# A hybrid encoder layer on one core: rows of a block's inverse dealt out in turn, two more merge columns computed in pairs, two output half columns begun early

## The chip, the core and the metric

The kernel runs on one core of a Trainium2 chip as one program. The metric is device time of one launch in microseconds (us). The core's engines are TensorE (PE, with its weight loads as PEld), VectorE (DVE), ScalarE (ACT) and GpSimd (POOL); SyncE (SP) issues most of the transfers between the chip's memory and the core, POOL a few of them. Each engine works through its own list of instructions in order and waits for the others by semaphores, so an instruction that waits also holds up everything behind it on its engine.

## The reference, cut to what matters

One encoder layer over 512 prompt tokens and 8 sequences of 16 sample tokens, 640 tokens of 2048 channels in all:

```python
z = x @ w_in                         # columns: FoX q|k|v|f|gate, delta rule q|k|v|a|beta|gate, merge gates m_a|m_b
y_a = (fox_attention(...) * silu(gate_a)) @ w_out_fox
conv = silu(causal_conv4(qkv_b)); q_b, k_b = l2norm, v_b
o_b, s_new = gated_delta_chunked(q_b, k_b, v_b, g, beta, s0)    # 8 heads, solves (I + L) u = v by triangular_solve
y_b = (rms_norm(o_b) * silu(gate_b)) @ w_out_gdn
h = (sigmoid(m_a) * y_a + sigmoid(m_b) * y_b) @ w_out
x1 = layer_norm(alpha * x + h)
out = x1 + sigmoid(x1 @ w_pl_gate) * rms_norm(p @ w_pl_proj)
```

All of it is float32. The outputs are `out`, the new keys, values and forget values of the attention, and the new convolution and delta rule states.

## The kernel before

**Matmuls.** Every float32 product is made of three passes: each operand is split into a high part (`wh`, `xh`, rounded to the fast matmul's type) and a rest (`wl`, `xl`), and PE adds high by high, high by rest and rest by high. The 640 tokens are two halves of 320, so a column of 128 outputs over 2048 inputs costs 16 steps x 6 = 96 matmuls of 128x320 (`column`, `mm6`, lines 396 and 397). Two columns can instead be made together by `pair` (line 474), a Winograd scheme with 7 products where the plain one has 8: 7 x 8 x 3 = 168 matmuls instead of 192. `half=True` is the same scheme over half of the inputs: one column, 7 x 4 x 3 = 84 matmuls. Weights arrive by SP in tiles `wr`, ACT casts pieces of 128x512 to `wh` (line 329), and the rest `wl` is made by DVE (line 335), or, where `self.summed` is set and the column lies below `SUMMED`, by ACT (line 332, minus the source) and a transfer issued by POOL that adds the source in place (line 342). At most `PIECES` = 5 pieces are ready ahead of PE.

**The stages.** `front` makes the first columns and 25 pairs: gates, values, `FRONT` = 22 merge columns (11 pairs) and four heads' q and k. `phase_fox` is the attention of 8 heads. `phase_gdn` is the delta rule: per head three columns (q, v, k of the convolution) and `FILL[h]` further merge columns to give the delta rule time, the last head four of them. Behind the last head come the plain columns of `w_out_fox` (`PLAIN` = 4, each in two halves by `column(groups=((0, 8), (8, 16)))`), and eight half columns by `pair(half=True)`, n = 4 to 7, which need the sums and differences of the attention's outputs (`xf`, made by `form_sums` and `form_splits`, lines 1650 to 1676, from `ogr` tiles that SP loads). `tail` then makes the 16 half columns of `w_out_gdn` (`u` = 0 to 7, two halves each), `w_out`, the layer norm and the last gate.

**The delta rule of a head** is a chain of generators: `conv_silu`, `gdn` (transposes, line 913 first), `gdn_blocks` (inverts the 32x32 diagonal blocks row by row on DVE, lines 1004 and 1006: 31 rows, two instructions each over a tile `sx` of 80 lanes x 8 columns x 32; the lanes are 20 blocks x 4 groups of 8 columns, and the tile's start is an identity, `in_eye`; the result is stored in `xd` by one transfer, line 1012), `gdn_feed` (loads it as `u`, line 1023), `gdn_merge` (POOL copies at line 1033, matmuls at 1043 to 1072 that merge the blocks into 128x128 inverses `uu`), `gdn_chunks` (matmuls at 1196 to 1211 and 1168), `gdn_out` (line 1117; the last head's result `og` is split into `nop[15]`, an operand of step 7 of every half column of `w_out_gdn`).

**What sets the order.** The program is recorded by hand: while the columns' matmuls are issued, `tick` advances the generators, and a step is taken when a small model of the engines' times says that its inputs are there. `until(cond)` goes on ticking without a matmul until a condition holds. So the change moves small instructions against the matmuls everywhere behind it. PSUM has 8 banks: four of tag `g` for the wide columns, and in `phase_gdn` and `tail` four of tag `s` for everything small, in two pools that follow each other. Tiles of `tail` take the place of the tiles of `phase_gdn`.

Of the kernel before, what the change touches and what calls it, by code (L numbers as in the profile page):

```python
# [52 lines left out]
class Kernel:  # L53
# [7 lines left out]
    PIECES = 5  # L61
    FRONT = 32 - 3 - 7
    APART = 2, 3, 5, 6
    NG = 8
    PAIR0, PAIRS = 6, NG + 2 + FRONT // 2 + len(APART)
    BETWEEN = 3, 6
    FILL = 0, 0, 1, 0, 1, 0, 1, 4
    PLAIN = 4
# [129 lines left out]
    def plan(self):  # L198
# [54 lines left out]
        self.summed, self.adds = False, deque()  # L253
        self.SUMMED = n - 48

# [142 lines left out]

    def column(self, cols=1, each=None, groups=((0, 16),), after=None, base=None, done=None):

        c = self.col
        self.col += cols
        out = []
        for n0, n1 in groups:
            ps = [tuple(self.gps(x.stop - x.start) for x in self.cut) for _ in range(cols)]
            for s in range(n0, n1):
                if each:  # L410
                    each(s)
                self.w_ahead()
                for x in range(cols):
                    self.mm6(ps[x], self.wk(c + x, s), self.op[s if base is None else base + s - n0], s == n0, s == n1 - 1)
                if s % 4 == 3:
                    self.used += cols
                if after:
                    after(s)
                self.tick()
            out += ps  # L420
            if done:
                done(ps[0])
        return out
# [564 lines left out]
    def gdn_blocks(self, h, kq, lt, qk, qg, kt, vr, cs):  # L988

        nc = self.nc  # L990
        for a in range(4):
            sl = slice(32 * a, 32 * a + 32)
            nc.sync.dma_start(out=self.ld[:, a].rearrange("t j i -> j t i"), in_=lt[sl, :, sl])
        yield 5
        x = self.zt([80, 8, 32], "sx")
        nc.sync.dma_start(out=x.rearrange("p c i -> p (c i)"), in_=self.i["eye"])
        lanes = self.zt([80, 32, 32], "lanes")
        nc.sync.dma_start(out=lanes.rearrange("p j i -> p (j i)"),
                          in_=bass.AP(self.ld.tensor, self.ld.offset, [[1024, 20], [0, 4], [1, 1024]]))
        yield 5  # L1000
        tmp = self.zt([80, 8, 32], "sx2")
        for j in range(31):
            n = 31 - j
            nc.vector.tensor_tensor(out=tmp[:, :, 0:n], in0=x[:, :, j:j + 1].to_broadcast([80, 8, n]),  # L1004
                                    in1=lanes[:, j:j + 1, j + 1:32].to_broadcast([80, 8, n]), op=ALU.mult)
            nc.vector.tensor_tensor(out=x[:, :, j + 1:32], in0=x[:, :, j + 1:32], in1=tmp[:, :, 0:n], op=ALU.subtract)  # L1006
            if j % 2 == 1:
                yield -1
        self.inv = h
        while self.fed < h - 2:  # L1010
            yield
        nc.sync.dma_start(out=self.xd[h % 2], in_=x.rearrange("p c i -> p (c i)"))
        self.feeds["gens"].append(self.gdn_feed(h, kq, lt, qk, qg, kt, vr, cs))
# [207 lines left out]
    def run(self, ctx):  # L1221
# [31 lines left out]
        with tc.manual_schedule():  # L1253
            with tc.tile_pool(name="ps2f", bufs=3, space=bass.MemoryType.PSUM) as self.ps2:
                with tc.tile_pool(name="zs", bufs=1) as self.zp:
                    self.front(work)
                with tc.tile_pool(name="zf", bufs=1) as self.zp:
                    self.phase_fox(work)
            with tc.tile_pool(name="ps2g", bufs=4, space=bass.MemoryType.PSUM) as self.ps2, \
                    tc.tile_pool(name="cs2", bufs=1) as c2, tc.tile_pool(name="zg", bufs=1) as self.zp:  # L1260
                self.cvst = c2.tile([P, 24, 24], F32, name="cvst")
                nc.sync.dma_start(out=self.cvst, in_=self.i["conv"])
                self.nbanks = 4
                self.phase_gdn(conv, work)
            with tc.tile_pool(name="ps2b", bufs=4, space=bass.MemoryType.PSUM) as self.ps2, \
                    tc.tile_pool(name="zb", bufs=1) as self.zp:
                self.tail()

# [306 lines left out]
    def phase_gdn(self, conv, work):  # L1575
# [76 lines left out]
        def form_sums(k, step):  # L1652

            a, b = fr[2 * k], fr[2 * k + 1]
            for o, x, y, op in ((b[:, xb], b[:, xb], a[:, xb], ALU.subtract), (a[:, xb], a[:, xb], a[:, xa], ALU.subtract),
                                (a[:, xa], b[:, xb], a[:, xa], ALU.add), (b[:, xa], b[:, xa], a[:, xa], ALU.subtract)):
                nc.vector.tensor_tensor(out=o, in0=x, in1=y, op=op)
            yield step
# [19 lines left out]
        def forms():  # L1678
# [11 lines left out]
            load2(3, "sg")  # L1690
            yield from form_splits(0, 3)
            load2(4, "ws")
            load2(5, "dt")
            yield from form_sums(1, 3)
            yield from form_splits(1, 3)
            load2(6, "v")
# [44 lines left out]
        for n in range(self.PLAIN, 8):  # L1741
# [16 lines left out]
            self.nf += 2  # L1758
        store()
        self.until(lambda: self.gdone == 7)  # L1760
        nop[15] = self.split(self.last)
# [81 lines left out]
    def tail(self):  # L1843
# [94 lines left out]
        for u in range(8):  # L1938
# [22 lines left out]
            def after(s):  # L1961
                if u == 7 and s in (6, 14):
                    odds(s // 14)
                if u == 7 and s == 12:
                    next(last7)
            self.column(groups=((0, 8), (8, 16)), base=8, each=each, after=after, done=gated)

# [365 lines left out]
def _consts():  # L2333
# [20 lines left out]
    smask[16:32] = 0.0  # L2354
    eye = np.zeros((20, 4, 8, 32), np.float32)
    for c in range(4):
        for j in range(8):
            eye[:, c, j, 8 * c + j] = 1.0
    return cb, smask, eye.reshape(80, 256)
# [114 lines left out]
```

## Time and profile before

| | |
|---|---|
| three timed runs | 2170.36, 2175.85, 2176.83 us (median 2175.85) |
| the profiled execution's own time | 2173.18 us |
| its span, first to last instruction | 2171.3 us |
| busy: PE, PEld, DVE, ACT, POOL | 99%, 96%, 72%, 46%, 19% |
| granted TensorE clock | 0.999 |
| instructions | 41951 |

By stage (us from the span's start): `front` runs to about 722, the attention to about 1010, the delta rule with the half columns of `w_out_fox` from there to 1636.5, `tail` to the end. In the profile's rows "out<-in" names the tiles written and read, "x" counts instructions, and "idle before" is the time in which the engine stood still just ahead of them, with what ended it.

### The profile page before, as it was taken

What the parts mean: (1) busy time and instruction counts of PE and PEld (TensorE: products, weight loads), DVE (VectorE), ACT (ScalarE), POOL (GpSimd) and SP (SyncE); (2) the same over time, 40 slices, a digit from 0 to 9 for tenths busy, and PEclk for the clock granted to TensorE, in tenths of its full rate; (3) what the DMA queues carried; (4) which work ended last, traced back from release to release, by engine and by line L of the source; (5) the groups of instructions that cost most, each with busy time, mean ns of one, the idle gap of its engine ahead of it and who ended that gap; (6) DMA issues with size and microseconds to landing.
All of it is one profiled execution on the core that took longest, in us unless ns stands there. A gap on an engine that the chain in (4) does not pass through costs nothing.

```text
span 2171.3 us, 41951 instructions
## 1 busy us (share of the span) xinstructions
PE 2149.0 (99%) x15438; PEld 2082.3 (96%) x15438; DVE 1566.0 (72%) x3207; ACT 1007.3 (46%) x2213; POOL 401.9 (19%) x596
## 2 busy tenths in 40 slices
PE   9999999999999999999999999999999999999998
PEld 7799999999999998899999999999999999999998
DVE  5877776767776565566478677766757787789987
ACT  4344443443444343353655566655443343354544
POOL 0022233323330101002334333332000000021100
PEclk9999999999999999999999999999999999999999
DMA  6356656666554899869978778878567656673465
GB/s 235 101 184 202 189 182 199 198 199 194 184 180 158 276 325 344 314 199 291 241 179 199 180 188 194 189 182 248 161 229 260 209 171 202 201 276 122 153 227 173
DMA packets 240670, 452.65 MB, mean 208 GB/s; under 512 B 38920, under 2 KB 122504, under 8 KB 240464
## 3 DMA queue, kind: packets, MB, share of 16 engines
q1 hardware_dynamic: 224912, 421.64, 59.5%
q0 software_dynamic: 15552, 28.32, 8.0%
q8 instruction: 122, 2.00, 0.4%
q14 instruction: 84, 0.69, 0.1%
HBM read 353.48 MB, written 96.38 MB: 207 GB/s over the span
## 4 chain that ended last, share of the span: by engine, by line
PE 91%; DVE 3%; DMA 3%; ACT 1%; SPq 0%; issue 0%; POOL 0%; ACTq 0%; DVEq 0%; POOLq 0%
PE g L474 44%; PE g L396 18%; PE g L397 18%; PE g L440 2%; PE s L974 1%; PE s L742 1%; PE s L813 1%; PE s L773 1%; DMA ws138b<-ws 0%; PE s L440 0%; PE s L1168 0%; DMA nb<-rd 0%; DVE sx L1006 0%; DVE sx L1004 0%; PE s L726 0%
## 5 line engine op out<-in xcount | busy, mean ns | idle before, releaser
L329 ACT CAST wh<-wr 128x512 fp32r<-128x512 f32 x624 | 381.2, 619 | 288.7 <-PE g L474 109.5
L335 DVE TENSOR_TENSOR wl<-wr,wh 128x512 fp32r<-128x512 f32 x516 | 358.3, 708 | 183.5 <-ACT wh L329 173.7
L474 PE MATMUL g<-xh,wh 128*128 128x320 f32 (+1 forms) x1296 | 402.9, 311 | 2.7 <-ACT m L1278 1.6
L474 PE MATMUL g<-xl,wh 128*128 128x320 f32 (+1 forms) x1296 | 401.2, 310 | 0.6 <-DVE xl L371 0.6
L474 PE MATMUL g<-xh,wl 128*128 128x320 f32 (+1 forms) x1296 | 401.4, 310 | 0.0
L396 PE MATMUL g<-xh,wh 128*128 128x320 f32 (+1 forms) x960 | 313.0, 326 | 0.7 <-ACT wh L329 0.7
L396 PE MATMUL g<-xh,wl 128*128 128x320 f32 (+1 forms) x960 | 297.1, 309 | 0.8 <-DMA wl<-in_w 0.7
L396 PE MATMUL g<-xl,wh 128*128 128x320 f32 (+1 forms) x960 | 297.2, 310 | 0.4 <-DVE xl L371 0.4
L397 PE MATMUL g<-xh,wh 128*128 128x320 f32 x960 | 297.3, 310 | 0.0
L397 PE MATMUL g<-xl,wh 128*128 128x320 f32 x960 | 297.0, 309 | 0.0
L397 PE MATMUL g<-xh,wl 128*128 128x320 f32 x960 | 296.7, 309 | 0.0
L474 PEld LDWEIGHTS g<-xh,wh 128*128 128x128 f32 x1296 | 243.9, 188 | 4.3 <-ACT m L1278 2.1
L474 PEld LDWEIGHTS g<-xl,wh 128*128 128x128 f32 x1296 | 243.7, 188 | 1.1 <-DVE xl L371 1.1
L474 PEld LDWEIGHTS g<-xh,wl 128*128 128x128 f32 x1296 | 244.1, 188 | 0.0
L474 PE MATMUL g<-t,wh 128*128 128x320 f32 (+1 forms) x1088 | 241.4, 310 | 0.0
L335 DVE TENSOR_TENSOR wl<-sr,wh 128x512 fp32r<-128x512 f32 x200 | 147.9, 759 | 98.6 <-ACT wh L329 97.6
L295 POOL TENSOR_TENSOR ws<-ws 128x171 f32<-128x171 f32 (+2 forms) x152 | 116.7, 768 | 541.5 <-DMA ws<-in_w 535.7
L396 PEld LDWEIGHTS g<-xh,wh 128*128 128x128 f32 x960 | 180.9, 188 | 11.9 <-issue 7.1
L474 PEld LDWEIGHTS g<-t,wh 128*128 128x128 f32 x1088 | 181.9, 188 | 0.6 <-issue 0.3
L396 PEld LDWEIGHTS g<-xh,wl 128*128 128x128 f32 x960 | 180.6, 188 | 1.4 <-DMA wl<-in_w 1.0
L397 PEld LDWEIGHTS g<-xh,wh 128*128 128x128 f32 x960 | 181.0, 189 | 0.9
L396 PEld LDWEIGHTS g<-xl,wh 128*128 128x128 f32 x960 | 180.9, 188 | 1.0 <-DVE xl L371 1.0
(440 smaller groups left out, 4148.8 us busy)
## 6 DMA issues: line engine op xcount, KB each, us to landing
wr<-in_w SPq DMA_DIRECT2D x252, 512.0 KB
wl<-in_w POOLq DMA_DIRECT2D x108, 256.0 KB, 5.8
kc<-in_kc SPq DMA_DIRECT2D x32, 512.0 KB
vc<-in_vc SPq DMA_DIRECT2D x32, 512.0 KB
sr<-in_w SPq DMA_DIRECT2D x25, 512.0 KB
ws<-in_w SPq DMA_DIRECT2D x96, 128.0 KB
sb<-in_w SPq DMA_DIRECT2D x80, 128.0 KB
md<-m SPq DMA_DIRECT2D x32, 320.0 KB
```

Source lines behind the costliest of these rows:

```text
L295: nc.gpsimd.tensor_tensor(out=o, in0=x, in1=y, op=op)
L329: nc.scalar.copy(out=hi, in_=src)
L335: nc.vector.tensor_tensor(out=lo, in0=src, in1=hi.bitcast(F32), op=ALU.subtract)
L396: nc.tensor.matmul(ps[0], whl[w], xhl[o][:, a], start=(first and x == 0), stop=(last and x == 2))
L397: nc.tensor.matmul(ps[1], whl[w], xhl[o][:, b], start=(first and x == 0), stop=(last and x == 2))
L440: nc.tensor.matmul(ps, x[:, sl], w, start=(s == 0 and n == 0), stop=(s == 15 and n == 2))
L474: nc.tensor.matmul(ps, a[:, w], b, start=(k == 0 and n == 0 and not more), stop=(k == last and n == 2), skip_group_check=True)
L742: nc.tensor.matmul(ops[:, 0:P], vn[:, kb, :], pT[:, kb * P:(kb + 1) * P], start=(kb == 0), stop=(kb == i))
L773: nc.tensor.matmul(s1[32 * j:32 * j + 32, :], self.qpad[:, 2 * j + par, :], kc[:, (j % 2) * NPT:(j % 2 + 1) * NPT], start=(par == 0), stop ...
L813: nc.tensor.matmul(od[32 * j:32 * j + 32, 0:P], self.ppad[:, c, 2 * j + par, :], vc[:, o:o + P], start=False, stop=(par == 1 and c == 3), ...
L974: nc.tensor.matmul(pp[:, o:o + 256].rearrange("p (a b) -> p a b", a=2), kq[:, 0, x], kq[:, :, x], start=True, stop=True)
```

## The change

- `FRONT` goes from 22 to 24: one more pair of merge columns in `front`, two `FILL` columns fewer in the delta rule, and the fills stand behind other heads (before: one behind heads 2, 4, 6 and four behind head 7; now one behind heads 3 and 5 and three behind head 7). `SUMMED` takes the four `PLAIN` columns in.
- `gdn_blocks`: the identity and the store deal a block's columns to the four lane groups in turn (column 4j + c instead of 8c + j), so that at row j only the first j // 4 + 1 columns of each lane can be other than zero, and the instructions cover only these. The store to `xd` becomes four transfers of 160 pieces of 128 bytes where there was one of 80 pieces of 1024 bytes.
- `form_sums` runs on POOL instead of DVE, and the waits between the first form steps go from 3 to 2 ticks.
- At the end of `phase_gdn`, behind the last pair and ahead of the wait for the last head, the first column of `w_out_gdn` is begun: steps 0 to 6 of its two halves, 2 x 42 matmuls, in the four `g` banks. `tail` ends them with step 7 (2 x 6 matmuls) in place of its column `u` = 0, and the first half of `u` = 1 takes two `s` banks. For this the pool of the `s` banks spans both stages.

```diff
-    FRONT = 32 - 3 - 7
+    FRONT = 32 - 3 - 5
-    FILL = 0, 0, 1, 0, 1, 0, 1, 4
+    FILL = 0, 0, 0, 1, 0, 1, 0, 3
-        self.SUMMED = n - 48
+        self.SUMMED = n - 44
...
-            ps = [tuple(self.gps(x.stop - x.start) for x in self.cut) for _ in range(cols)]
+            if banks:
+                ps, banks = [tuple(t[:, 0:x.stop - x.start] for t, x in zip(banks, self.cut))], ()
+            else:
+                ps = [tuple(self.gps(x.stop - x.start) for x in self.cut) for _ in range(cols)]
...
-                          in_=bass.AP(self.ld.tensor, self.ld.offset, [[1024, 20], [0, 4], [1, 1024]]))
+                          in_=bass.AP(self.ld.tensor, self.ld.offset, [[0, 4], [1024, 20], [1, 1024]]))
...
-            nc.vector.tensor_tensor(out=tmp[:, :, 0:n], in0=x[:, :, j:j + 1].to_broadcast([80, 8, n]),
-                                    in1=lanes[:, j:j + 1, j + 1:32].to_broadcast([80, 8, n]), op=ALU.mult)
-            nc.vector.tensor_tensor(out=x[:, :, j + 1:32], in0=x[:, :, j + 1:32], in1=tmp[:, :, 0:n], op=ALU.subtract)
+            m = j // 4 + 1
+            nc.vector.tensor_tensor(out=tmp[:, 0:m, 0:n], in0=x[:, 0:m, j:j + 1].to_broadcast([80, m, n]),
+                                    in1=lanes[:, j:j + 1, j + 1:32].to_broadcast([80, m, n]), op=ALU.mult)
+            nc.vector.tensor_tensor(out=x[:, 0:m, j + 1:32], in0=x[:, 0:m, j + 1:32], in1=tmp[:, 0:m, 0:n],
+                                    op=ALU.subtract)
...
-        nc.sync.dma_start(out=self.xd[h % 2], in_=x.rearrange("p c i -> p (c i)"))
+        xd = self.xd[h % 2]
+        for a in range(4):
+            nc.sync.dma_start(out=bass.AP(xd.tensor, xd.offset + 32 * a, [[1024, 20], [128, 8], [1, 32]]),
+                              in_=x[20 * a:20 * a + 20])
...
-                nc.vector.tensor_tensor(out=o, in0=x, in1=y, op=op)
+                nc.gpsimd.tensor_tensor(out=o, in0=x, in1=y, op=op)
...
-            yield from form_splits(0, 3)
+            yield from form_splits(0, 2)
...
+        c, self.begun = self.col, []
+        for n in range(2):
+            ps = tuple(self.gps() for _ in range(2))
+            for s in range(8 * n, 8 * n + 7):
+                self.w_ahead()
+                self.mm6(ps, self.wk(c, s), nop[8 + s % 8], s % 8 == 0, False)
+                if s % 8 == 3:
+                    self.used += 1
+                self.tick()
+            self.begun.append(ps)
         self.until(lambda: self.gdone == 7)
...
-            self.column(groups=((0, 8), (8, 16)), base=8, each=each, after=after, done=gated)
+            if u == 0:
+
+                for n, ps in enumerate(self.begun):
+                    self.w_ahead()
+                    self.mm6(ps, self.wk(self.col, 8 * n + 7), self.op[15], False, True)
+                    self.used += 1
+                    each(8 * n)
+                    each(8 * n + 3)
+                    gated(ps)
+                self.col += 1
+                continue
+            self.column(groups=((0, 8), (8, 16)), base=8, each=each, after=after, done=gated,
+                        banks=[self.sps() for _ in range(2)] if u == 1 else ())
...
-            eye[:, c, j, 8 * c + j] = 1.0
+            eye[c, :, j, 4 * j + c] = 1.0
```

Where the sums stand. Before, DVE near the end of the last head's inversion (`sx`), the last two of the four groups of sums (`ogr<-ogr`, four instructions each) with the splits (`xl`, `t`) and weight rests (`wl`) around them:

```order
L335 TENSOR_TENSOR wl<-wr,wh 128x512
L1657 TENSOR_TENSOR ogr<-ogr 128x320 x4
L371 TENSOR_TENSOR xl<-ogr,xh 128x640
L1669 TENSOR_TENSOR t_19137<-ogr,t_19137 128x320
L1004 TENSOR_TENSOR sx_18486<-sx,lanes 80x8
L1006 TENSOR_TENSOR sx<-sx,sx_18486 80x8
L335 TENSOR_TENSOR wl<-wr,wh 128x512
L1669 TENSOR_TENSOR t_19138<-ogr,t_19138 128x320
L1657 TENSOR_TENSOR ogr<-ogr 128x320 x4
L371 TENSOR_TENSOR xl<-ogr,xh 128x640
```

Now, POOL at that place, all four groups of sums (line 1664 of the changed kernel), with the last two heads' small work (`vm`, the copies to `uu` that the last merge needs, `kpad`, `gpad`) and the adding weight transfers (`wl<-in_w`) between them:

```order
L1664 TENSOR_TENSOR ogr<-ogr 128x320 x4
L1160 TENSOR_TENSOR vm<-vnd,cb 128x256
L342 DMA wl<-in_w 128x512 x2
L1041 COPY uu_11559<-u_18996 32x5x32 x4
L1664 TENSOR_TENSOR ogr<-ogr 128x320 x4
L342 DMA wl<-in_w 128x512 x3
L1094 COPY kpad<-kqs 128x4x16 x2
L1094 COPY gpad<-gr 128x4x16 x2
L1664 TENSOR_TENSOR ogr<-ogr 128x320 x8
```

The sums have left DVE's list, where the last ones stood behind nearly all of the inversion; on POOL the last two groups follow each other, and the merge's copies and the weight transfers stand behind sums.

Where `tail` begins. Before, PE at step 7 of the first half column of `w_out_gdn` (`xh_20185` and `xl_20186` are the last head's split), in banks `g_20204` and `g_20205`, and the next half column behind it:

```order
L396 MATMUL g_20204<-xh_20185,wh_20113 128x320
L397 MATMUL g_20205<-xh_20185,wh_20113 128x320
L396 MATMUL g_20204<-xl_20186,wh_20113 128x320
L397 MATMUL g_20205<-xl_20186,wh_20113 128x320
L396 MATMUL g_20204<-xh_20185,wl_20114 128x320
L397 MATMUL g_20205<-xh_20185,wl_20114 128x320
L396 MATMUL g_20276<-xh_20050,wh_20135 128x320
```

Now, PE at the same operand (`xh_20333`): the ends of both begun half columns, and behind them the second column's first half in `s` banks:

```order
L396 MATMUL g_20229<-xh_20333,wl_20158 128x320
L397 MATMUL g_20230<-xh_20333,wl_20158 128x320
L396 MATMUL g_20283<-xh_20333,wh_20206 128x320
L397 MATMUL g_20284<-xh_20333,wh_20206 128x320
L396 MATMUL g_20283<-xl_20334,wh_20206 128x320
L397 MATMUL g_20284<-xl_20334,wh_20206 128x320
L396 MATMUL g_20283<-xh_20333,wl_20207 128x320
L397 MATMUL g_20284<-xh_20333,wl_20207 128x320
L396 MATMUL s_20384<-xh_20094,wh_20231 128x320
L397 MATMUL s_20385<-xh_20094,wh_20231 128x320
```

The last head's operand is now first used 84 matmuls after the last pair where it was 42, and all four `g` banks are full until `tail` has read them.

Where an inverse is stored. Before, SP's rows for the last head, the store to `xd` and the load of `u` three rows later:

```order
L1012 DMA xd_135<-sx 80x256
L269 DMA wr<-ws102S_196 128x1024
L1712 DMA fd_18669<-fx 128x640
L1023 DMA u_19211<-xd_135 128x5x32
L269 DMA wr<-ws102b 128x1024
```

Now, the same place on SP:

```order
L1628 DMA ogr<-ogd_71 128x640
L1019 DMA xd_135<-sx 160x1x32 x4
L1031 DMA u_18996<-xd_135 128x5x32
L269 DMA wr<-in_w 128x1024
```

The store is four rows, and the load of `u` follows at once, with the weight loads behind it.

More of the change, by code (lines that the diff above doesn't have):

```diff
@@ L397, in mm6, with column @@
             nc.tensor.matmul(ps[1], whl[w], xhl[o][:, b], start=(first and x == 0), stop=(last and x == 2))
-    def column(self, cols=1, each=None, groups=((0, 16),), after=None, base=None, done=None):
+    def column(self, cols=1, each=None, groups=((0, 16),), after=None, base=None, done=None, banks=()):
         c = self.col
@@ L1258, in run @@
                     self.phase_fox(work)
[L1259 to L1267, printed above, removed]
+            with tc.tile_pool(name="ps2g", bufs=4, space=bass.MemoryType.PSUM) as self.ps2:
+                with tc.tile_pool(name="cs2", bufs=1) as c2, tc.tile_pool(name="zg", bufs=1) as self.zp:
+                    self.cvst = c2.tile([P, 24, 24], F32, name="cvst")
+                    nc.sync.dma_start(out=self.cvst, in_=self.i["conv"])
+                    self.nbanks = 4
+                    self.phase_gdn(conv, work)
+                with tc.tile_pool(name="zb", bufs=1) as self.zp:
+                    self.tail()
     def values(self, g, temp, after=None):
@@ L1690, in forms @@
             load2(3, "sg")
-            yield from form_splits(0, 3)
+            yield from form_splits(0, 2)
             load2(4, "ws")
             load2(5, "dt")
-            yield from form_sums(1, 3)
-            yield from form_splits(1, 3)
+            yield from form_sums(1, 2)
+            yield from form_splits(1, 2)
             load2(6, "v")
@@ L2354, in _consts @@
     smask[16:32] = 0.0
-    eye = np.zeros((20, 4, 8, 32), np.float32)
+    eye = np.zeros((4, 20, 8, 32), np.float32)
     for c in range(4):
         for j in range(8):
-            eye[:, c, j, 8 * c + j] = 1.0
+            eye[c, :, j, 4 * j + c] = 1.0
     return cb, smask, eye.reshape(80, 256)
```

## The prediction

> **What bounds the kernel now.** I read the page's head first, then the windows by stage, two windows of plain columns, and the waits. The head, with busy time, share and instructions of each engine:
>
> ```profile
> span 2171.3 us, 41951 instructions
> PE 2149.0 (99%) x15438; PEld 2082.3 (96%) x15438; DVE 1566.0 (72%) x3207; ACT 1007.3 (46%) x2213; POOL 401.9 (19%) x596
> ```
>
> PE is busy for all but 22.3 us. The windows (start:end and length, then PE, PEld, DVE, ACT and POOL, clock, DMA share, GB/s) are two stretches of plain columns, then the delta rule with the half columns, and the tail:
>
> ```profile
> 150.00:200.00 50.00, 50.00 (x343) 50.00 (x341) 39.13 (x50) 20.97 (x38) 17.11 (x16) 1.00 0.58 185
> 1700.00:1750.00 50.00, 50.00 (x342) 50.00 (x341) 39.10 (x70) 15.94 (x29) 0.00 (x0) 1.00 0.59 198
> 1010.00:1637.00 627.00, 621.93 (x4732) 597.43 (x4732) 434.48 (x1331) 356.58 (x964) 182.60 (x310) 1.00 0.79 203
> 1637.00:2150.00 513.00, 512.36 (x3466) 510.21 (x3466) 418.51 (x721) 225.72 (x393) 28.99 (x64) 1.00 0.60 203
> ```
>
> Without gaps PE passes 343 matmuls in 50 us, one in 50 / 343 = 0.146 us, at a clock of 1.00. The delta rule's 627 us hold only 627.0 - 621.9 = 5.1 us without PE, and the tail 0.6. So a matmul that goes is worth 0.146 us, a wait that goes can bring 5.1 us at most, and the rest of the change counts only where it makes PE wait. The longest waits of PE (line <- what released it: us, times, longest):
>
> ```profile
> PE s L1196 <- DVE uu L1074: 1.9, 1, 1.9
> ...
> PE s L1072 <- issue: 0.9, 2, 0.7
> ...
> PE s L1168 <- DVE S L1206: 0.9, 1, 0.9
> ...
> PE g L396 <- DMA wl<-in_w: 0.7, 1, 0.7
> ...
> PE g L474 <- DVE fx L483: 0.6, 1, 0.6
> ```
>
> **Fewer matmuls.** Two columns go from 2 x 96 = 192 matmuls to a pair of 168: 24 fewer, 24 x 0.146 = **-3.5 us**. The begun half columns are moved, neither added nor saved (84 + 12 is a column's 96). A pair also costs sums of weights and inputs on DVE, where 39.1 of 50 us are busy, so they lie beside PE. The matmul rows must not set the price:
>
> ```profile
> L474 PE MATMUL g<-xh,wh 128*128 128x320 f32 (+1 forms) x1296 | 402.9, 311 | 2.7 <-ACT m L1278 1.6
> ```
>
> Its mean is 311 ns with a start every 146, so records overlap, and 24 x 0.311 would make 7.5. [...]
>
> **The rows of the inverse.** All eight heads' solves (x, then busy and mean ns, then DVE's idle time before them), with the first and the last row of one by their widths:
>
> ```profile
> L1004 DVE TENSOR_TENSOR sx<-sx,lanes 80x248 f32<-80x248 f32 (+30 forms) x248 | 75.4, 304 | 16.5 <-DMA lanes<-ld 11.4
> L1006 DVE TENSOR_TENSOR sx<-sx,sx 80x248 f32<-80x248 f32 (+30 forms) x248 | 76.3, 308 | 8.5
> ...
> L1004 DVE TENSOR_TENSOR sx<-sx,lanes 80x248 f32<-80x248 f32 x8 | 3.3, 408 | 11.4 <-DMA lanes<-ld 11.4
> L1006 DVE TENSOR_TENSOR sx<-sx,sx 80x24 f32<-80x24 f32 x8 | 1.4, 180 | 0.3
> ```
>
> From 248 to 24 elements the time falls by 228 ns, 1.02 ns an element. An instruction's elements over a head's 31 rows sum to 8 x (31 + ... + 1) = 3968 before and to the sum of (j // 4 + 1)(31 - j) = 1560 now. That is 2408 x 1.02 = 2.5 us each and 4.9 us a head off (75.4 + 76.3) / 8 = 19.0: 39 us of DVE. On PE it is worth nothing by itself; it can shorten one wait, this one (start, duration, engine, instruction, [wait]):
>
> ```profile
> 1437.38 0.41 DVE L1004 TENSOR_TENSOR sx<-sx,lanes 80x248 f32<-80x248 f32 x1 [5.58 <-DMA lanes<-ld]
> ...
> 1447.01 0.42 DVE L1074 TENSOR_SCALAR uu<-s 64x256 f32<-64x256 f32 x1
> 1447.48 0.49 PE L1196 MATMUL s<-vr,uu 128*128 128x128 f32 x2 [1.92 <-DVE uu L1074]
> ```
>
> DVE starts the next head's solve less than 10 us before PE wants the `uu` of the one ahead; shorter steps there bring between 0 and 1.9 us. But the same stage loses two plain columns, 192 x 0.146 = 28 us of matmuls that gave every head time: 39 us of DVE against 28 us of PE, spread otherwise over the heads. The waits come between all gone (-5.1) and some more; I take 0.
>
> The store is four issues instead of one:
>
> ```profile
> L1012 SPq DMA_DIRECT2D xd<-sx x8: 330/334/341, 1116.6 to 1555.0; - x8
> L1023 SPq DMA_DIRECT2D u<-xd x8: 370/384/490, 1119.9 to 1560.2; - x8
> ```
>
> Three more issues are 3 x 0.334 = 1.0 us a head. Behind them SP holds the load of `u`, for which the merge waits, and weight loads, which PE wants only pieces later. The 640 short pieces are what the load of `u` already reads; landing is bounded by 0 and another load's way, 1560.2 to 1567.3 for the last head. A shorter solve (4.9 us) pays most of that. I take 0.
>
> **The sums on POOL.** Before, on DVE, with POOL's two nearest forms and their spread (min/median/max ns, first and last start):
>
> ```profile
> L1657 DVE TENSOR_TENSOR ogr<-ogr 128x320 f32<-128x320 f32 x16 | 8.1, 505 | 0.5
> ...
> L295 POOL TENSOR_TENSOR ws<-ws 128x171 f32<-128x171 f32 x80 | 54.6, 683 | 32.5 <-DMA ws<-in_w 28.3
> L295 POOL TENSOR_TENSOR ws<-ws 128x256 f32<-128x256 f32 x56 | 52.1, 930 | 507.0 <-DMA ws<-in_w 506.0
> ...
> L295 POOL TENSOR_TENSOR ws<-ws x152: 481/737/1761, 119.7 to 1490.0; 128x171 f32<-128x171 f32 x80, 128x256 f32<-128x256 f32 x56, 128x169 f32<-128x169 f32 x16
> ```
>
> By the means, (930 - 683) / 85 = 2.9 ns an element, so 128x320 is about 0.930 + 64 x 0.0029 = 1.12 us; the bounds are 481 x 320 / 171 = 0.9 and 1761 x 320 / 256 = 2.2. DVE loses 8.1 us and POOL gains 16 x 1.12 = 18 over hundreds of us. What matters is the way to the first half pair:
>
> ```profile
> L1669 DVE TENSOR_TENSOR t<-ogr,t x8: 481/484/492, 1524.5 to 1560.9; 128x320 fp32r<-128x320 f32 x8
> ...
> 1578.05 0.31 PE L474 MATMUL g<-xh,wh 128*128 128x320 f32 x1
> ```
>
> The last split ends at 1561.4, so its slack is 16.7 us. Between the last head's start (line 913) and the first half pair the order has 672 wide matmuls before and 594 after: 78 x 0.146 = 11.4 us less. The last two groups of sums take 8 x (1.12 - 0.51) = 4.9 longer. Waits between form steps fall by a tick seven times, 6 matmuls each: 7 x 0.88 = 6.1 back. About 6.5 us are left, and PE waits for nothing; behind it stand the merge's copies on POOL, with the same slack.
>
> **Weight rests.** Sixteen pieces of `w_out_fox` leave DVE for ACT and a POOL transfer, and eight of the fills' go:
>
> ```profile
> L335 DVE TENSOR_TENSOR wl<-wr,wh 128x512 fp32r<-128x512 f32 x516 | 358.3, 708 | 183.5 <-ACT wh L329 173.7
> ...
> L332 ACT ACTIVATE wl<-wr 128x512 fp32r<-128x512 f32 x108 | 68.6, 636 | 0.0
> ...
> L342 POOL DMA_DIRECT2D wl<-in_w x108 | 94.5, 881 | 200.9 <-ACT wl L332 162.9 <-ACT junk L935 12.6 <-ACT vn L1198 7.6
> ...
> wl<-in_w POOLq DMA_DIRECT2D x108, 256.0 KB, 5.8
> ```
>
> A piece costs ACT 0.64, POOL 0.88 and then 5.8 us to land, and five pieces are ahead, 5 x 24 x 0.146 = 17.5 us of plain columns; it is late only when POOL holds it for over 17.5 - 5.8 - 0.6 - 0.9 = 10 us, as two groups of sums standing together (8 x 1.12 = 9.0) nearly do. ACT has 627 - 357 = 270 us free in the stage. I take 0, bounds 0 and one piece's lateness, about 2 us.
>
> **The begun column.** With all four banks held, the next wide matmuls need them free. The last pair and the first gated half column are:
>
> ```profile
> 1636.53 0.32 PE L396 MATMUL g<-xh,wh 128*128 128x320 f32 x1
> ...
> 1642.12 0.32 SPq L1863 DMA_DIRECT2D t<-fd  x1
> 1645.87 0.82 DVE L1945 SCALAR_TENSOR_TENSOR t<-t 128x640 f32<-128x640 f32 x1 [4.79 <-DMA t<-md]
> ...
> 1647.67 0.89 DVE L1870 SCALAR_TENSOR_TENSOR t<-t,g 128x320 f32<-128x320 f32 x2 [0.38 <-DMA t<-md]
> ```
>
> The first half column is read by 1648.6, 12.0 us after the pairs, since `tail` must load `md` and `fd` first. Now the `g` banks are wanted again behind 84 begun matmuls (12.3), 12 ends (1.8) and the 48 that use `s` banks (7.0): 21.1 us. That leaves 9.0 us if the loads are issued as early; if they wait for all 12.3 us of begun work, PE waits 3.3. Between 0 and 3.3 I take 0. Nor does this part bring much: before, step 7 found the last head's split with at most 0.6 us of PE waits.
>
> **The sum.** -3.5 + 0 on the profiled execution's 2173.2 is **2169.7 us**. That run lies 2.7 below the median of the three shown.
>
> **The rivals.**
>
> *The waits go too.* DVE is lighter by 39 + 8 + 16 x 0.71 = 58 us from the stage's 434, so `uu`, `S` and `fx` come earlier: the five waits above, 1.9 + 0.9 + 0.9 + 0.7 + 0.6 = 5.0, go: 2169.7 - 5.0 = 2164.7. For it: three of the five end on DVE. Against: 28 us fewer matmuls to hide behind, and each fix shows the next latest thing. Chance 0.20.
>
> *The begun column eats the gain.* The 84 matmuls hide nothing, since the last head is done by then, and the held banks cost 3.3: 2173.0. The change then doesn't do what it is laid out for. Against: 9.0 us of margin if the loads go early. Chance 0.12.
>
> *The sums are slow on POOL.* [...] At 2.2 us the sixteen take 16 x 1.08 = 17.3 us more; 6.5 to 7 are slack, PE waits about 10.5, and the time is 2169.7 + 10.5 = 2180.2. PE starts to wait at 1.12 + 6.5 / 16 = 1.5 us a sum, and the kernel is slower than before from 1.5 + 3.5 / 16 = 1.75. Against: the means of the same instruction, 0.93 over 56. Chance 0.08. [...]
>
> **How the numbers follow.** Forecast 0.60, and 0.20, 0.12, 0.08. The range is 2163 to 2178: down to the waits gone and 1.7 of spread between runs; up to +2.7 for the median, +3.3 for the banks and +2 for a late piece. 0.3%, 6.5 us, is about what a measurement can tell from no change. From the profiled 2173.2 only the first rival passes it (-8.5) and only the last on the other side (+7.0): faster 0.20, same 0.72, slower 0.08.
>
> **What would show it.** Right: 24 wide matmuls fewer, the solve's two lines near 14 us a head, sums near 1.1 us, PE's waits between 1010 and the end of the pairs near 5 us again, and no wait of `g` matmuls in the tail's first 25 us. Wrong: sums over 1.5 us with PE idle ahead of the first half pair, or `L396` in the tail waiting for its banks, or waits of the merge for a late `u`.

## The result, and the profile after

| | before | changed |
|---|---|---|
| median | 2172.67 us (6 runs, 2170.36 to 2176.83) | 2187.88 us (6 runs, 2184.04 to 2190.17) |
| ratio, 95% interval | | 1.0066, 1.0050 to 1.0081 |
| profiled execution, its span | 2173.18, 2171.3 us | 2190.17, 2188.4 us |
| clock | 0.999 | 0.994 |

The change makes the kernel 0.66% slower, some 15 us, where 3.5 us less had been forecast. The head of the page, then the delta rule with its half columns (to the last pair at 1654.2) and the tail, in the changed kernel. With one more pair in `front` the delta rule starts 24.5 us later, so the first 25 us of the first window belong to the attention; PE has no gap in them:

```profile
span 2188.4 us, 41992 instructions
PE 2153.5 (98%) x15414; PEld 2083.5 (95%) x15414; DVE 1528.3 (70%) x3198; ACT 1014.8 (46%) x2228; POOL 420.6 (19%) x620
...
1010.00:1654.20 644.20, 625.24 (x4702) 597.70 (x4702) 400.75 (x1328) 362.23 (x978) 204.56 (x342) 0.98 0.82 208
1654.20:2150.00 495.80, 495.17 (x3351) 493.03 (x3351) 404.02 (x698) 215.42 (x377) 28.87 (x64) 1.00 0.60 203
```

PE has its 24 matmuls fewer, and the tail has 0.6 us without PE as before. The stage between has 644.2 - 625.2 = 19.0 us without PE instead of 5.1, at a clock of 0.98. The waits of PE (us in total, times, longest):

```profile
PE s L1074 <- DVE t L1060: 12.9, 2, 10.7
PE g L477 <- DVE fx L486: 1.6, 1, 1.6
PE g L477 <- ACT m L1285: 1.6, 1, 1.6
PE g L396 <- DMA wl<-in_w: 1.5, 1, 1.5
```

One wait is new and bigger than all that were there: the merge's matmuls (line 1074) wait for DVE's `t` (line 1060), twice. DVE at the longer one, then PE, then SP before it:

```profile
1533.07 0.19 DVE L1008 TENSOR_TENSOR sx<-sx,lanes 80x31 f32<-80x31 f32 x1 [15.09 <-DMA lanes<-ld]
1533.30 0.19 DVE L1010 TENSOR_TENSOR sx<-sx,sx 80x31 f32<-80x31 f32 x1
1533.52 0.19 DVE L1008 TENSOR_TENSOR sx<-sx,lanes 80x30 f32<-80x30 f32 x1
1533.74 0.19 DVE L1010 TENSOR_TENSOR sx<-sx,sx 80x30 f32<-80x30 f32 x1
1533.96 0.28 DVE L1060 TENSOR_SCALAR t<-s 32x128 f32<-32x128 f32 x1
```

```profile
1534.30 1.11 PE L1074 MATMUL s<-t,lt 64*64 64x64 f32 x8 [10.69 <-DVE t L1060]
1535.34 0.63 PE L396 MATMUL g<-xh,wh 128*128 128x320 f32 x1
```

```profile
1515.35 2.42 SPq L996 DMA_DIRECT2D ld<-lt  x4
...
1523.49 1.76 SPq L291 DMA_DIRECT2D ws<-in_w  x4
1525.30 0.42 SPq L999 DMA_DIRECT2D sx<-in_eye  x1
1525.77 0.67 SPq L1001 DMA_DIRECT2D lanes<-ld  x1
```

DVE stands 15.1 us at the first row of the last head's inversion, since its `lanes` are issued at 1525.77, 8.0 us behind the last store of their source, and come 7.3 us after that. Two rows on stands the step of the merge of the head before; its input, PE's matmuls of 1520.4, had been there for 12 us, and PE waits for it. Nothing in this is slow: the order of DVE's list, fixed when the program is recorded, has the row ahead of the merge, five ticks behind an issue whose data take 7 us; and DVE came to the row at 1518.0, before SP had even issued the load. In the kernel before, the last head's first row (line 1004 there) stood behind that merge (line 1052), with no wait for lanes:

```profile
1487.28 0.28 DVE L1052 TENSOR_SCALAR t<-s 32x128 f32<-32x128 f32 x1 [4.11 <-PE s L1051]
...
1502.21 0.40 DVE L1004 TENSOR_TENSOR sx<-sx,lanes 80x248 f32<-80x248 f32 x1
```

The second head's first row stands 3.8 us likewise, with PE's other wait of 2.3 us behind it. Over the heads:

```profile
L1008 DVE TENSOR_TENSOR sx<-sx,lanes 80x60 f32<-80x60 f32 (+24 forms) x248 | 55.8, 225 | 35.9 <-DMA lanes<-ld 30.0
L1010 DVE TENSOR_TENSOR sx<-sx,sx 80x60 f32<-80x60 f32 (+24 forms) x248 | 54.9, 221 | 8.5
```

An inversion costs (55.8 + 54.9) / 8 = 13.8 us, but DVE stands for lanes 30.0 us where it stood 11.4. Last, the stretches behind the two waits; the clock is the last number but two:

```profile
1160.00:1170.00 10.00, 10.00 (x46) 9.43 (x45) 8.98 (x38) 3.95 (x11) 5.07 (x12) 0.52 0.85 230
1534.00:1540.00 6.00, 5.70 (x33) 5.32 (x34) 5.24 (x24) 0.37 (x1) 0.00 (x0) 0.65 0.58 131
```

After each of these two waits PE goes on at half the clock, 0.50 in windows of 0.25 us up to 1169.6 and 1538.2. Three of its rows behind the short one:

```profile
1161.23 0.47 PE L396 MATMUL g<-xl,wh 128*128 128x320 f32 x1
1161.50 0.47 PE L397 MATMUL g<-xl,wh 128*128 128x320 f32 x1
1161.77 0.47 PE L396 MATMUL g<-xh,wl 128*128 128x320 f32 x1
```

A wide matmul every 0.267 us instead of 0.146: 29 of them behind the short wait, 29 x 0.12 = 3.5 us lost, and 0.9 with the merge's two small groups among them; 11 behind the long one, 1.3 + 0.5. The two waits with their half clock make 2.3 + 10.7 + 4.4 + 1.8 = 19.2 us. The account is of the two profiled executions, whose spans differ by 17.1 us: PE is without work for 34.9 us instead of 22.3, 12.6 more; the half clock costs 6.2 instead of some 1.5 in the kernel before, 4.7 more; the matmuls take 3.5 off. That is 13.8, so some 3 us of this one execution are not found.

### The profile page after: what moved, and what is told of

It is laid out like the page before. It is cut to its first block, busy times and chain, and to the rows that moved or that the text cites. A ratio compares the mean times of both kernels' runs of the same rounds, so it can differ in the third digit from the quotient of the medians.

```text
span 2188.4 us, 41992 instructions
## 1 busy us (share of the span) xinstructions
PE 2153.5 (98%) x15414; PEld 2083.5 (95%) x15414; DVE 1528.3 (70%) x3198; ACT 1014.8 (46%) x2228; POOL 420.6 (19%) x620
## 4 chain that ended last, share of the span: by engine, by line
PE 87%; DMA 5%; DVE 5%; ACT 1%; SPq 1%; issue 1%; POOL 0%; ACTq 0%; DVEq 0%; POOLq 0%
PE g L477 45%; PE g L396 16%; PE g L397 15%; PE g L443 2%; DVE sx L1010 1%; DVE sx L1008 1%; DMA lanes<-ld 1%; PE s L745 1%; PE s L816 1%; PE s L776 1%; PE s L977 1%; DVE cy L883 1%; DMA ld<-lt 0%; PE s L443 0%; DMA ws138b<-ws 0%
## 5 line engine op out<-in xcount | busy, mean ns | idle before, releaser
L335 DVE TENSOR_TENSOR wl<-wr,wh 128x512 fp32r<-128x512 f32 x506 | 353.6, 713 | 178.2 <-ACT wh L329 173.1
L397 PE MATMUL g<-xh,wh 128*128 128x320 f32 x920 | 285.8, 311 | 0.0
L397 PE MATMUL g<-xl,wh 128*128 128x320 f32 x920 | 285.4, 310 | 0.0
L397 PE MATMUL g<-xh,wl 128*128 128x320 f32 x920 | 284.8, 310 | 0.0
L477 PEld LDWEIGHTS g<-xh,wh 128*128 128x128 f32 x1328 | 250.0, 188 | 5.3 <-ACT m L1285 2.1
L396 PEld LDWEIGHTS g<-xh,wh 128*128 128x128 f32 x920 | 174.2, 189 | 13.1 <-issue 7.3
L329 ACT CAST wh<-sr 128x512 fp32r<-128x512 f32 x208 | 125.1, 618 | 132.6 <-PE g L477 105.2
```

What stands on the lines that cost most here:

```text
L329: nc.scalar.copy(out=hi, in_=src)
L335: nc.vector.tensor_tensor(out=lo, in0=src, in1=hi.bitcast(F32), op=ALU.subtract)
L396: nc.tensor.matmul(ps[0], whl[w], xhl[o][:, a], start=(first and x == 0), stop=(last and x == 2))
L397: nc.tensor.matmul(ps[1], whl[w], xhl[o][:, b], start=(first and x == 0), stop=(last and x == 2))
L477: nc.tensor.matmul(ps, a[:, w], b, start=(k == 0 and n == 0 and not more), stop=(k == last and n == 2), skip_group_check=True)
```

## The experiments

Three theories: **standing** (in-order engines stand for a load that the recorded order leaves no time for, with urgent steps behind; its first form, **order**, blames only the place of a head's first row ahead of the earlier head's merge), **store** (the four transfers of an inverse) and **cover** (with two columns fewer, PE has too little to do between a head's steps). Each ratio is to the kernel before on the same chip, with its 95% interval; the change itself has 1.0066.

**The first row behind the merge.**

```
         yield 5
+        while self.merged < h - 1:
+            yield
         tmp = self.zt([80, 8, 32], "sx2")
```

> The changed kernel, in which the first row of a head's inversion is recorded only when the merge of the head before it has come to its last matmuls; all else as changed. Order theory: what costs the time is that DVE, in order, stands at the second and at the last head's first row until its lanes have landed, with the earlier head's merge behind it; with the merge in front both of PE's waits for the merge (2.3 and 10.7 us) go and the half clock behind them (about 4.6 and 1.4 us): 2188 - 19 = 2169, at most 2173. Store theory (the four transfers of the inverse hold up SP): the waits stay, 2184 to 2190. Cover theory (two columns fewer and fills at other heads leave PE without work there): the wait moves to another instruction and the time stays within 4 us of 2188.

1.0067 (1.0052 to 1.0082), 2189.8 us. The order theory as put there fails: PE's waits for line 1060 are gone, and two others have come, here with DVE's rows:

```profile
PE s L1206 <- DVE rp L1202: 6.2, 1, 6.2
PE s L1206 <- DVE uu L1084: 5.5, 1, 5.5
```

```profile
1461.52 0.19 DVE L1010 TENSOR_TENSOR sx<-sx,lanes 80x31 f32<-80x31 f32 x1 [5.39 <-DMA lanes<-ld]
...
1526.78 0.19 DVE L1010 TENSOR_TENSOR sx<-sx,lanes 80x31 f32<-80x31 f32 x1 [8.03 <-DMA lanes<-ld]
```

DVE still stands at first rows, only now `rp` (with a stand of 4.7 us for another load, `gr`, between) and the last `uu` are behind them. So it isn't this pair of instructions; it is the standing, whatever comes next in the list.

**The lanes sooner, the lists of the engines unchanged.**

```
-        yield 5
+        yield 3
         x = self.zt([80, 8, 32], "sx")
...
-        yield 5
+        yield 7
         tmp = self.zt([80, 8, 32], "sx2")
```

> The changed kernel, in which the identity and the lanes are asked for two ticks sooner and the first row follows two ticks later behind them, so that DVE's, PE's and ACT's lists stay word for word the same and only SP's differs (for the last head the two loads go ahead of four weight loads whose buffers come free late). Order theory: the lanes of the last head land 3 to 5 us sooner and PE's longest wait falls from 10.7 to 6 to 8 us, and the second head's short one goes or halves: 2178 to 2185. Store theory: no change, since the store stands where it stood. Cover theory: no change or a little.

1.0054 (1.0038 to 1.0070), 2186.2 us; the profiled execution is at the lower end, span 2179.2. Its longest wait of PE is 5.8 us, and DVE stands 9.3 us at the last head: as far as the lanes come sooner, PE's wait shrinks. The gain in the median is inside the intervals.

**The lanes kept.** Lanes are loaded for the first head only, so seven heads' inverses are computed from the first head's rows; the identity is loaded ahead of `ld`.

```
+        if h == 0:
+            self.lanes0 = self.zt([80, 32, 32], "lanes")
+        lanes = self.lanes0
+        if h == 0:
             nc.sync.dma_start(out=lanes...)
```

> The changed kernel in which the lanes are loaded for the first head only and used for all eight (the other heads' inverses are computed from the first head's rows), and the identity is loaded ahead of the lanes' source; the lists of PE, DVE, ACT and POOL are those of the changed kernel word for word. So no first row waits for a load that is just under way. Standing theory (DVE stands at a first row for a load that takes 7 us where the list allows five ticks, and whatever is behind it, merge or other, is late): all of DVE's waits for lanes go, 30 us, PE's two waits for the merge too: 2168 to 2172. Store theory: the waits for the merge stay or move by 3 us: 2180 or more. Cover theory (PE has too little to do between the heads' steps): 2180 or more, with other waits of PE in place of these.

> The same edit on the kernel before (the other heads' inverses from the first head's rows). Its DVE waits for lanes are 11.4 us, and PE waits 1.9 us behind one of them with 1.2 us of half clock after it: 2169 to 2173 by the standing theory, about 3 us under the kernel before; the difference to the changed kernel with the same edit is then what the change is worth without these waits, -3.5 by the count of matmuls. Store and cover theory: the same 0 to 3 us here.

The change with it: 1.0010 (0.9997 to 1.0022), 2174.7 us. Before with it: 0.9983 (0.9973 to 0.9992), 2168.8 us. The lists of PE, DVE, ACT and POOL are the same, no row waits for lanes behind the first head, and the changed kernel is 13 us faster. The same edit takes 4 us off the kernel before, which had such waits too; so of the 15.2 us between the two, 6.0 are left and 9 hang on the loads of the lanes: that part of the standing is shown. (The edit also takes seven loads off SP; this isn't told apart from their lateness.) The changed kernel still lies 6 us above the other where its matmuls should put it 3.5 below; some 9 us are something else. The profiled execution of the changed kernel with this edit is the slowest of its ten, 2180.7 us, so its trace shows more waits than the median has.

**The parts alone.** The change with full rows and one store (without_dealing), and the kernel before with nothing but the dealing (dealing_alone) or nothing but `FRONT` and `FILL` (columns_alone).

> The changed kernel with the inversion as before: full rows, the old identity, one store per head. Store theory: the loss goes, 2165 to 2170. Order theory: the first eight instructions of the last head's inversion still stand ahead of the merge in DVE's list, and its lanes still come nine or so issues behind their source on SP, so PE waits there again: 2180 or more. Cover theory: 2180 or more too.

> The kernel before with nothing but the dealt rows, the identity dealt and four stores a head. Store theory: slower than before, 2180 or more, with waits of PE for the merge. Order theory: the first row stands ahead of the merge for the second and the fifth head only, and the last heads have it behind: within 5 us of before, 2168 to 2178, with a wait at the fifth head if its lanes are late. Cover theory: as before, 2170 to 2174.

> The kernel before with two more merge columns in front, two fewer behind heads and the rest of the fills as in the change, nothing else. By the count of matmuls 2170. Standing theory: the first row of the last head stands ahead of the merge of the one before it, as without the dealing: one wait of 3 to 6 us and its half clock, 2174 to 2184. Cover theory: 2180 to 2190, waits at several heads. Store theory: 2168 to 2172.

All three are slower: 1.0040 (1.0025 to 1.0055), 1.0089 (1.0074 to 1.0104) and 1.0081 (1.0066 to 1.0096). The two parts cost 21 and 17 us alone and 15 together, so they don't add up. In without_dealing the last head's first row still stands ahead of the merge, and DVE waits 7.8 us at it (15.1 in the change) and PE 3.7 us behind it; three other waits of 2.3 to 4.5 us are new. In columns_alone the row stands there too, but DVE comes to it late and waits for nothing. So the row's place at the last head comes from the moved columns and not from the dealing. The dealing alone waits where the standing theory put it, at the second and the fifth head, but far longer than I expected:

```profile
PE s L1071 <- DVE t L1057: 8.8, 2, 4.7
PE s L1201 <- DVE uu L1079: 3.3, 1, 3.3
```

```profile
1127.65 0.19 DVE L1005 TENSOR_TENSOR sx<-sx,lanes 80x31 f32<-80x31 f32 x1 [6.09 <-DMA lanes<-ld]
...
1316.51 0.19 DVE L1005 TENSOR_TENSOR sx<-sx,lanes 80x31 f32<-80x31 f32 x1 [6.71 <-DMA lanes<-ld]
```

The columns alone wait elsewhere, in the last head's chain:

```profile
PE s L1188 <- DVE S L1206: 6.3, 3, 2.6
PE s L1117 <- ACT ob L1112: 5.4, 1, 5.4
```

Line 1117 of the last head comes 1650.7 - 1465.2 = 185 us after its line 913 there, behind the last pair, where it took 1623.6 - 1454.2 = 169 before. Two further kernels keep the lanes of the first head in these two (again with seven heads' inverses from the first head's rows):

> dealing_alone (the kernel before with nothing but the dealt rows and the four stores), with the lanes loaded for the first head only and the identity ahead (seven heads' inverses from the first head's rows). It was 20.7 us slower than before. Standing theory: all three of its long waits stood behind lanes that were under way, so 2168 to 2174. Store theory: the four stores are still there, and so is most of the loss: 2185 to 2195.

> columns_alone (the kernel before with two more merge columns in front and two fewer behind heads), with the lanes loaded for the first head only and the identity ahead (seven heads' inverses from the first head's rows). It was 16.7 us slower than before, with PE's waits in the last head's chain and only 2 to 4 us stood by DVE for lanes. Standing theory as the cause of everything: 2168 to 2174. Cover theory (the last head's chain with full rows is longer than what PE still has to do): 2182 to 2190, the waits at the last head as they were.

The dealing falls to 1.0025 (1.0015 to 1.0034), 16 us less. Beside the kernel before with the same edit it lies 9.9 us higher instead of 20.7, so about half of its loss was standing for lanes. The columns stay at 1.0070 (1.0056 to 1.0084), with PE's 5.4 us in the last head's chain as it was: their loss isn't the lanes, and by these waits it is cover, at the last head. In the change the last head's line 1125 comes 1633.2 - 1466.0 = 167 us after its transposes, ahead of the last pair's end, so by its trace this cover loss isn't in it, and the standing is.

**One store.** The dealt inverse is stored by one transfer as before, so its columns lie permuted.

> The changed kernel with one store of the inverse as before in place of four (the inverse's columns then lie in the dealt order, so the outputs that rest on them are of permuted columns); the lists of PE, DVE, ACT and POOL are the change's. Store theory: the 2.7 us that SP gains for each head and the earlier load of u take the loss away, 2170 to 2176. Standing theory: the lanes are late by what stands between them and their source on SP, not by the store of the head before; 2182 to 2189, 1 to 4 us gained at most.

> dealing_kept (dealt rows on the kernel before, lanes of the first head for all) with one store instead of four, so nothing is left of the dealing but shorter rows in their own places in the lists. dealing_kept is 10 us above before_lanes_kept. If the four stores are what is left: 2168 to 2172. If it is the order of the lists: 2175 to 2180.

1.0059 (1.0047 to 1.0072) for the change, with DVE's 13.8 us at the last head and PE's 9.4 us behind it as they were; 1.0012 (1.0003 to 1.0021) for the dealing with kept lanes. The store theory fails as the cause; what the four stores cost is 1 to 3 us by the medians, within the intervals.

**The first row later.** Eleven ticks behind the lanes instead of five (rows_later); and, with the identity ahead and the lanes at three ticks, ten ticks, with 24 and with 22 columns in front.

> The changed kernel, complete, in which the first row follows eleven ticks behind the lanes' issue instead of five, so that the lanes should have landed. DVE's list then has the first row behind the merge for all heads but the second. Standing theory: DVE's waits for lanes fall from 30 us to under 10, PE's longest wait to under 3: 2170 to 2176. Store and cover theory: the chain of a head gets longer by 5 us, and other waits of PE come instead: 2184 to 2195.

> The same edit of the rows on the change as it is (24 in front). Standing theory alone: 2168 to 2172, below its twin by the 3.5 us of 24 matmuls. Cover theory: above its twin, 2175 to 2182, with PE's waits at the last two heads. Store theory: 2180 to 2190.

> The changed kernel with 22 merge columns in front and the fills of before (so 24 matmuls more than the change), the identity ahead of the lanes' source, the lanes two ticks sooner and the first row ten ticks behind them. Dealing, sums on POOL and begun columns as in the change. Standing theory with the cover theory as its second half (two columns of matmuls hide the heads' chains again): DVE hardly waits for lanes and PE neither, 2168 to 2174. Store theory: 2180 to 2190, since the four stores are there.

1.0033 (1.0022 to 1.0045), 1.0046 (1.0031 to 1.0062) and 1.0096 (1.0081 to 1.0111). The first takes half of the loss away; in its profiled execution, the fastest of eight, DVE stands 4.9 us for lanes and PE's longest wait is 1.8, as expected, but the median stays 4 us above the expected range. In the second DVE still stands 12.2 us. The third was expected at before's time and is, by its ratio, the slowest of all. There DVE hardly stands for lanes any more, but for other loads that the order has no time for. DVE and POOL in it:

```profile
1127.85 1.40 DVE L943 SCALAR_TENSOR_TENSOR dt<-gr,colT,cb 128x128 f32<-128x128 f32 x5 [6.41 <-DMA gr<-rd]
...
1562.72 0.85 DVE L371 TENSOR_TENSOR xl<-ogr,xh 128x640 fp32r<-128x640 f32 x1 [9.95 <-ACT xh L370]
1563.48 0.30 DVE L1043 STREAM_TRANSPOSE m<-u 128x128 f32<-128x128 f32 x1
```

```profile
1558.27 3.66 POOL L1664 TENSOR_TENSOR ogr<-ogr 128x320 f32<-128x320 f32 x4 [8.38 <-DMA ogr<-ogd]
```

POOL stands for the attention's `ogr`, ACT for POOL's sum, DVE for ACT's `xh`, and the last merge (line 1043) behind that: PE waits 6.9 us. The standing isn't a matter of the lanes alone.

**The rest of the change.** Without the begun columns, and the change with kept lanes (seven heads from the first head's rows) and the sums back on DVE:

> The changed kernel without the begun half columns (the first column of w_out_gdn is made whole in the tail, as before). The loss lies ahead of the last pair by the traces so far, and the lists up to there are the same: by every theory within 3 us of the changed kernel, 2185 to 2191. If the begun columns had cost or brought something, 2184 or less, or 2191 or more.

> As lanes_kept (seven heads' inverses from the first head's rows), with the sums of the half columns on DVE again as before. lanes_kept is 6 us above before_lanes_kept. If POOL's list is what stays over (vm stood behind four sums, and PE waited 2.9 us for it): that wait goes, 2169 to 2172. If what stays over is the shorter stage (cover theory), 2173 to 2177 with waits elsewhere.

1.0063 (1.0047 to 1.0080) and 1.0005 (0.9991 to 1.0020; lanes_kept has 1.0010). The begun columns make no difference that can be told. With the sums on DVE the 2.9 us wait for `vm` is gone, and waits of 3.5 us for `rp` and 3.1 us for `m` are there; nothing is gained that can be told.

**The kernel before with the lanes sooner.** Identity first, lanes at three ticks, the row where it was.

> The kernel before, complete, with the identity loaded ahead of the lanes' source and the lanes two ticks sooner, the first row where it was: the lists of PE, DVE, ACT and POOL are those of before. Standing theory: DVE's 5.6 us wait at the seventh head falls to 1 to 3, PE's 1.9 us behind it and its half clock (1.2) go: 2169 to 2172, 1 to 4 us faster than before. Store and cover theory: no difference that can be told.

0.9985 (0.9976 to 0.9994), 2170.6 us: the fastest complete kernel here, 2.6 us under before. Its seventh head:

```profile
1431.19 0.41 DVE L1004 TENSOR_TENSOR sx<-sx,lanes 80x248 f32<-80x248 f32 x1 [0.93 <-DMA lanes<-ld]
```

where 5.58 us stood, and PE's 1.9 us for `uu` is gone.

## Why the prediction was wrong

**The step that failed** is in the part on the rows of the inverse: "The waits come between all gone (-5.1) and some more; I take 0." The lower end had a price and the upper end none, and the time went there: 12.9 us of waits and 6.2 us lost at half clock behind them. The rest of that part weighed budgets, 39 us of DVE against 28 us of PE, and a wait doesn't come from budgets. It comes from which instruction stands in front of which. The row I quoted there, `[5.58 <-DMA lanes<-ld]`, was the mechanism itself: DVE stood for a load, and PE's 1.9 us followed. I read it as a long solve in the way, which shorter steps could only shorten. Shorter rows bring DVE to the next load sooner, where it stands longer (at the last head 15.1 us, and 7.8 with full rows in without_dealing), and they put each later step elsewhere in the list. The moved columns, whose effect I had taken as cover alone, put the last head's row ahead of the earlier head's merge, which it wasn't before. Taking away the standing for lanes takes 9 of the 15 us away (lanes_kept beside before_lanes_kept).

**The matmuls**, -3.5: PE has 24 fewer, and its plain columns run at the same pace (177 matmuls from 1654.2 to 1680.0, 0.146 us each as before); the gain is there under the loss.

**The solve**, 14 us a head: 13.8. The size was right, and off the path.

**The store**, 1.0 us more of SP a head: each of the four issues takes longer than the old one, so it is 3.0 - 0.33 = 2.7:

```profile
L1019 SPq DMA_DIRECT2D xd<-sx x32: 747/758/864, 1135.3 to 1553.4; - x32
```

Taking it as free was nearly right all the same: 1 to 3 us by the medians (one_store), within the intervals. The merge did wait, but for DVE's `t` and not for a late `u`, which was the sign I had named.

**The sums on POOL**, 1.12 us, bounds 0.9 and 2.2: 15.3 / 16 = 0.95, and no wait of PE ahead of the first half pair.

```profile
L1664 POOL TENSOR_TENSOR ogr<-ogr 128x320 f32<-128x320 f32 x16 | 15.3, 954 | 11.5 <-DMA xd<-sx 5.1 <-DMA ogr<-ogd 4.5 <-DVE st L1181 1.0
```

The rival of slow sums is out; the spread of 481 to 1761 ns behind its 2.2 us was over three widths of instruction, 128x169 to 128x256. What they bring instead is POOL's standing for `ogr` and `xd`, which is in the list's order again.

**The weight rests**, 0 to 2: PE's wait for them is 1.5 us instead of 0.7.

**The begun columns**, 0 to 3.3: 0. PE has no wait of note in the tail (0.6 us in 496), and leaving them out changes nothing that can be told.

**The rivals and the range.** The rival with a gain looked at PE's waits in the right stage and had the sign wrong; the wait that came, the merge for `t`, wasn't among its five. The slow rival had its place on POOL, and I gave no rival to a DVE that stands for a load. The range ended at 2178 because its upper end left out that term.

**Open** stay some 9 us of the change with kept lanes (2174.7, against 2168.8 - 3.5), and about 8 of the dealing with kept lanes and one store (2176.6 against 2168.8). Their traces show waits of 1 to 3 us at several places, and the clock of their profiled executions is 0.998 and 0.999 (0.999 in the kernel before with kept lanes); I tried no kernel that takes them all away. Nor is it shown why an order with more time for lanes and 22 columns does worse than one with 24: its waits are named, but not what put them there.

## What to carry to other kernels

Where a program's order is recorded by hand, an edit that only shortens work off the path still reorders every list behind it; ask of each load which engine will stand at its first reader, for how long by the trace (issue to use), and what is queued behind that reader. A bound of "some more" on waits needs a price as well: the longest standing in the trace of before plus the clock that PE loses after it. Here that would have been 5.6 us and half clock, and still too little: the load that cost most was issued only 7.8 us after DVE had come to it. Where the order of a changed kernel can be seen, look for first readers of loads that have moved ahead of steps PE wants.

## What the runs showed of the hardware

In the changed kernel a wait of 2.3 us was followed by about 10 us at half clock, and one of 10.7 us by about 4 us; so the shorter wait cost 2.3 + 4.4 = 6.7 us. In the kernel before, the clock fell to 0.50 behind a wait of 1.9 us:

```profile
1448.00:1451.00 3.00, 3.00 (x13) 3.00 (x13) 2.90 (x8) 2.16 (x4) 0.17 (x1) 0.50 1.08 275
```

Read in windows of 0.25 us, the granted clock of these two kernels is 1.00 or 0.50, but for the windows in which it changes. Between 1010 and 1654 us the changed one has two slow stretches, which begin at 1159.36 and 1527.99 and last 10.24 us each; the one before has one, which begins at 1448.03 and lasts 3.41. PE had stood for 2.1 us of the 3.41 us ahead of the first fall and for 1.9 us of the 3.41 ahead of that in the kernel before; a wait of 1.65 us in the changed kernel (up to 1639.79) brought no fall. What a wait cost here didn't follow from its length alone: the clock fell 4.4 us into the long wait, and 6.3 us of its slow stretch passed while PE stood anyway, where it fell 0.2 us before the end of the short one. Why the short wait's stretch lasted 10.24 us and that of the kernel before 3.41 isn't shown; the first 3.41 us and the second each hold a group of eight 64x64 matmuls of 1.1 us, the third none.

A transfer of 160 pieces of 128 bytes took SP 0.76 us to issue, and one of 80 pieces of 1024 bytes 0.33.
